# Six of eight blocks of the second feed-forward product by seven half-size products in each layer

## The chip, the cores and the metric

One core of one Trainium2 chip. The metric is the device time of one execution in microseconds (us). TensorE is called PE here, VectorE DVE, ScalarE ACT, GpSimd POOL, SyncE SP, as the profile calls them.

## The reference

Two layers over 512 tokens of width 1024. Each layer is a normalised projection, a pooling mixer and an indexed attention, an output projection, and then the feed-forward part, which is the part that matters here:

```python
D_FF = 4 * D_MODEL          # 1024 -> 4096 -> 1024
for l in range(DEPTH):      # DEPTH = 2
    ...
    x = x + rms_norm(mix, g_post_mix[l])
    h = rms_norm(x, g_pre_ffn[l])
    f = jnp.square(jax.nn.relu(h @ w_ff1[l])) @ w_ff2[l]
    x = x + rms_norm(f, g_post_ffn[l])
```

All inputs are float32, and so is the output.

## The kernel before

**Exactness.** PE takes float32 rounded to a shorter form (fp32r). So every operand is kept as a high part (a copy that rounds) and a low part (the value minus the high part), and every product is three matmuls: high by high, high by low, low by high (`PASSES`, `mm3`). The high parts are copies, which either DVE or ACT may do (`copy`, a choice of the planner). The low parts are subtractions of two tensors, and `tt` gives those to DVE alone.

**Weights.** `WeightStream` loads weights in DMAs of 512 KB issued by SP, and makes tiles `ws` of high and low part from them, 128 rows by 512 columns each, in a ring of eight (`NWS`). A tile is refilled when the matmuls on it are over (`done`). Plain weights pass through `wraw` (two buffers), one copy and one subtraction a tile.

**The first feed-forward product** is cut into eight blocks of 512 hidden columns. Block 0 is a plain product (tiles `pf`). The other seven are done by seven half-size products instead of eight (`unit_products`): the 2 x 2 quarters of the weights (in `uraw`, two buffers of two quarters' worth) are combined into S1 to S4, the quarters of the activations into T1 to T4 (once a layer), and PE makes seven products into the banks `one` and `two`. For the weights of one block that is 14 tiles `ws`, so 14 copies and 14 subtractions, and 8 more additions and subtractions on DVE for S1 to S4 (tiles `usum` and `uraw`). The result of each quarter is squared after a relu (`fr`) and split into the parts of `f`, `f1h`, `f1l`.

**The second feed-forward product** is plain. Two blocks of hidden columns at a time (loop `g`, four times a layer) and for each half of the 1024 output columns, 8 chunks by 4 token tiles by 3 passes of 512 columns go into four banks `pg`, and DVE adds the banks into `facc` (the first time they are copied).

**Order.** Nothing runs in the order in which it is written. Every operation is recorded (`_Recorder`, line 372, which is why all rows of the profile carry that line), and `Planner.issue` puts the operations of each engine into a fixed order by rules on durations and latencies. On the chip each engine takes its instructions in that order and waits for semaphores.

Of the kernel before, what the change touches and what calls it, by code (L numbers as in the profile page):

```python
# [12 lines left out]
F32 = mybir.dt.float32  # L13
# [5 lines left out]
P = 128  # L19
# [16 lines left out]
NWS = 8  # L36
NRAW = 2
# [45 lines left out]
class Planner:  # L83
# [9 lines left out]
    DMA_LANDS = 1050  # L93
    CELL = 64
# [93 lines left out]
    def lag(self, ea, eb):  # L188
        if eb == "sp":
# [169 lines left out]
class _Recorder:  # L359
# [3 lines left out]
    def __getattr__(self, method):  # L363
        def call(*args, **kw):
# [4 lines left out]
            reads = [a for k, a in list(enumerate(args))[1:] + list(kw.items())  # L369
# [19 lines left out]
    def cost(self, method, args, kw, out, reads):  # L389
# [20 lines left out]
        if self.name == "pool":  # L410
            if method == "memset":
                return 50
            return (70 + 1.2 * n) if method == "tensor_scalar" else (520 if n == 1 else 50 + 2.35 * n)
        nbytes = math.prod(c for _, c in out.ap) * 4
# [3 lines left out]
class WeightStream:  # L418
# [5 lines left out]

    COMBINATIONS = ("11", "12", "S2", "S1", "S3", "S4", "22")

    def __init__(self, copy, tt, sp, raw_pool, ws_pool, unit_pool, sum_pool):
        self.copy, self.tt, self.sp = copy, tt, sp
# [53 lines left out]
    def _ahead(self):  # L482

        while self.n_load < len(self.loads):
            unit = self.loads[self.n_load][2] == "unit"
# [5 lines left out]
    def _load(self):  # L491
# [3 lines left out]
        if n == "unit":  # L495
# [43 lines left out]
    def _combine(self, k, name, w):  # L539
# [3 lines left out]

        def quarter(i, j):
            return raw[:, j, :, 256 * i:256 * i + 256]

        def v(ap):
            return ap.rearrange("p (c n) -> p c n", c=2)
# [37 lines left out]
def hymba_trunk(ctx: ExitStack, tc: tile.TileContext, x, positions, g_pre_mix, w_in, w_pool,  # L586
# [4 lines left out]
        ("pe", nc.tensor), ("act", nc.scalar), ("dve", nc.vector), ("pool", nc.gpsimd), ("sp", nc.sync))]  # L591
    ctx.enter_context(tc.manual_schedule())
# [72 lines left out]
    ws = WeightStream(copy, tt, sp, rawp, wsp, t8p, sup)  # L665
    plan = []
    for l in range(DEPTH):
# [14 lines left out]
        for g in range(4):  # L682
            for b in (2 * g, 2 * g + 1):
                p["ff1", b] = ws.add_unit(w_ff1[l], 0, 512 * b) if b else ws.add(w_ff1[l], 0, D, 512 * b, 512)
            for hf in range(2):
                p["ff2", g, hf] = ws.add(w_ff2[l], 1024 * g, 1024, 512 * hf, 512)
# [183 lines left out]
    for l in range(DEPTH):  # L870
# [261 lines left out]
        def unit_products(ids, f):  # L1132
# [21 lines left out]
            def evac(rows, cols, value, other=None):  # L1154
                r = t2("fr")[:, :512]
                if other is not None:
                    dve.tensor_tensor(r, value, other, op=OP.add)
                    value = r
                planner.either(lambda: act.activation(r, value, AF.Relu),
                               lambda: dve.tensor_scalar(r, value, 0.0, None, op0=OP.max))  # L1160
                squared(r, r)
                rv = r.rearrange("p (j n) -> p j n", j=2)
                hi = f[0][:, 2 * rows:2 * rows + 2, cols]
                copy(hi, rv)
                tt(f[1][:, 2 * rows:2 * rows + 2, cols], rv, hi.bitcast(F32), OP.subtract)
# [4 lines left out]
            evac(0, LATER, two, p1)  # L1170
# [6 lines left out]
            evac(1, SOONER, one, p5)  # L1177
            product(two, "S4", "22")
            evac(0, SOONER, two, u2)
            product(one, "22", "T4")  # L1180
            evac(1, LATER, one)

        facc = None
        for g in range(4):
            f1 = []
            for bi in range(2):
                blk = 2 * g + bi
                if bi == 0:
                    f = [c2a.tile([P, 4, S], F32R, name="f1h", tag="c2a"), c2b.tile([P, 4, S], F32R, name="f1l", tag="c2b")]
                else:  # L1190
                    f = c1p.tile([P, 2, 4, S], F32R, name="f1", tag="c1")
                    f = [f[:, 0], f[:, 1]]
                f1.append(f)
                ids = p["ff1", blk]

                def evac_f(j, ps, cols):
                    r = t2("fr")[:, :ps.shape[1]]
                    planner.either(lambda: act.activation(r, ps, AF.Relu),
                                   lambda: dve.tensor_scalar(r, ps, 0.0, None, op0=OP.max))
                    squared(r, r)  # L1200
# [3 lines left out]
                if blk == 0:  # L1204
                    for tp in (1, 0):
                        cols = slice(256 * tp, 256 * tp + 256)
                        for j in range(4):
# [70 lines left out]
```

## Time and profile before

| | us |
|---|---|
| median of 3 runs | 1189.85 (1188.28 to 1189.97) |
| profiled execution, its own time | 1189.19 |
| its span, first to last instruction | 1187.4 |
| outside the span | 1.8 |

PE is busy for 97% of the span, DVE for 81%, ACT for 50%, POOL for 3%; the mean granted PE clock is 0.992 of full speed. The feed-forward part lies at about 248 to 598 us in layer 0 and 834 to 1179 us in layer 1. In a timeline, two adjacent records of one engine can overlap: the start of the next one, not the length of a record, tells how fast the engine takes such instructions.

### The profile page before, as it was taken

How to read it: one execution, taken by the hardware profiler on the slowest of the kernel's cores; microseconds unless marked ns; L12 is line 12 of the kernel's file. 1: busy time of each engine (PE TensorE's matmuls, PEld its weight loads, DVE VectorE, ACT ScalarE, POOL GpSimd, SP SyncE). 2: the span in 40 equal slices, each digit the busy share in tenths (PEclk: the TensorE clock that was granted, in tenths of full speed). 3: DMA queues.
4: the chain of work that ended last, by engine and by line, in shares of the span. 5: the costliest groups of instructions: out<-in, count | busy, mean ns of one | idle time of the engine just before them, and what ended most of it. 6: DMA issues, size and time to landing. Idle time of an engine off the chain costs nothing.

```text
span 1187.4 us, 18436 instructions
## 1 busy us (share of the span) xinstructions
PE 1154.9 (97%) x6888; PEld 1008.9 (85%) x6888; DVE 962.8 (81%) x2134; ACT 593.5 (50%) x1279; POOL 31.5 (3%) x79
## 2 busy tenths in 40 slices
PE   6999999999999999999999999899999999999997
PEld 6988888789899898899898888777998998988985
DVE  7799999889569579577698999998994785875965
ACT  7545796687226036035275277876760440430621
POOL 2000000010000000000010000001000000000001
PEclk9999998999999999999999999999999999999999
DMA  7221222451423223223233121134542241251231
GB/s 249 71 72 36 71 72 72 142 184 66 161 74 132 95 72 132 82 71 97 60 112 89 54 72 54 54 115 134 160 141 73 71 161 54 72 177 36 72 107 71
DMA packets 62169, 115.55 MB, mean 97 GB/s; under 512 B 5248, under 2 KB 10368, under 8 KB 62080
## 3 DMA queue, kind: packets, MB, share of 16 engines
q1 hardware_dynamic: 62080, 114.38, 30.2%
q8 instruction: 54, 0.88, 0.3%
q14 instruction: 35, 0.29, 0.1%
HBM read 112.27 MB, written 2.10 MB: 96 GB/s over the span
## 4 chain that ended last, share of the span: by engine, by line
PE 61%; DVE 26%; DMA 5%; ACT 4%; issue 3%; POOL 1%; SPq 0%; DVEq 0%; ACTq 0%; POOLq 0%
PE pg L372 33%; PE one L372 9%; PE two L372 7%; DVE ws L372 6%; DVE bias L372 3%; PE pi L372 3%; PE pf L372 3%; DVE m L372 3%; DMA wraw<-in_w_out_dram 2%; DMA uraw<-in_w_ff_dram 2%; DVE mx L372 1%; PE lg L372 1%; DVE s L372 1%; PE po L372 1%; DVE pT L372 1%
## 5 line engine op out<-in xcount | busy, mean ns | idle before, releaser
L372 PE MATMUL pg<-ws,f 128*128 128x512 f32 x768 | 230.5, 394 | 0.0
L372 PE MATMUL pg<-ws,A 128*128 128x512 f32 x864 | 227.5, 401 | 0.9 <-DVE A L372 0.6
L372 ACT ACTIVATE ws<-wraw 128x512 fp32r<-128x512 f32 (+1 forms) x182 | 112.9, 632 | 183.8 <-PE pg L372 127.3
L372 DVE TENSOR_TENSOR ws<-wraw,ws 128x512 fp32r<-128x512 f32 (+1 forms) x288 | 194.4, 689 | 5.9 <-ACT ws L372 3.8
L372 PEld LDWEIGHTS pg<-ws,A 128*128 128x128 f32 x864 | 157.7, 188 | 34.3 <-DVE pn L372 1.6
L372 PE MATMUL pg<-ws,f1h 128*128 128x512 f32 x512 | 167.2, 394 | 0.5 <-ACT fr L372 0.5
L372 PEld LDWEIGHTS pg<-ws,f 128*128 128x128 f32 x768 | 141.1, 188 | 29.0
L372 PEld LDWEIGHTS pg<-ws,f1h 128*128 128x128 f32 x512 | 95.6, 188 | 22.3 <-ACT fr L372 1.0
L372 DVE TENSOR_TENSOR ws<-uraw,ws 128x512 fp32r<-128x512 f32 x168 | 111.7, 686 | 2.0 <-ACT ws L372 0.7
L372 DVE CAST ws<-wraw 128x512 fp32r<-128x512 f32 (+1 forms) x106 | 45.0, 426 | 75.2 <-PE pg L372 64.3
L372 PE MATMUL two<-A,ws 128*128 128x256 f32 x672 | 104.9, 281 | 0.0
L372 PE MATMUL pg<-ws,f1l 128*128 128x512 f32 x256 | 95.8, 393 | 0.0
L372 PEld LDWEIGHTS two<-A,ws 128*128 128x128 f32 x672 | 92.3, 188 | 1.9
L372 ACT ACTIVATE ws<-uraw 128x512 fp32r<-128x512 f32 x95 | 57.7, 627 | 67.8 <-PE pg L372 29.7
L372 ACT ACTIVATE s<-s,st 128x384 f32<-128x384 f32 (+3 forms) x118 | 64.7, 565 | 21.4 <-DVE st L372 20.8
L372 ACT ACTIVATE fr<-fr 128x512 f32<-128x512 f32 (+1 forms) x109 | 63.5, 596 | 21.0 <-DVE fr L372 20.1
L372 DVE TENSOR_TENSOR facc<-pg,facc 128x512 f32<-128x512 f32 x48 | 32.7, 688 | 46.2 <-PE pg L372 46.2
L372 DVE CAST ws<-uraw 128x512 fp32r<-128x512 f32 x73 | 30.4, 424 | 41.7 <-PE pg L372 32.6
L372 PE MATMUL pi<-ws,A 128*128 128x292 f32 x384 | 61.8, 310 | 1.1 <-DVE ws L372 0.8
L372 PE MATMUL pool<-A,ws 128*128 128x512 f32 x192 | 59.2, 405 | 0.0
L372 PEld LDWEIGHTS pg<-ws,f1l 128*128 128x128 f32 x256 | 48.0, 188 | 10.9
L372 PE MATMUL one<-A,ws 128*128 128x256 f32 x336 | 57.0, 280 | 0.0
(189 smaller groups left out, 2203.5 us busy)
## 6 DMA issues: line engine op xcount, KB each, us to landing
wraw<-in_w_ff_dram SPq DMA_DIRECT2D x72, 512.0 KB, 3.8
uraw<-in_w_ff_dram SPq DMA_DIRECT2D x56, 512.0 KB, 4.9
wraw<-in_w_out_dram SPq DMA_DIRECT2D x32, 512.0 KB, 3.7
wraw<-in_w_in_dram SPq DMA_DIRECT2D x24, 512.0 KB, 3.6
wraw<-in_w_in_dram SPq DMA_DIRECT2D x8, 584.0 KB, 4.3
wraw<-in_w_in_dram SPq DMA_DIRECT2D x16, 256.0 KB, 2.9
x<-in_x_dram SPq DMA_DIRECT2D x4, 512.0 KB, 6.5
out_dram<-x SPq DMA_DIRECT2D x8, 256.0 KB, 2.1
```

The lines of the kernel that those rows point to most:

```text
L372: lambda: getattr(self.real, method)(*args, **kw), self.port(method, out, reads))
```

## The change

In blocks 1 to 6 of each layer the second product is done by seven half-size products too; blocks 0 and 7 stay plain (`PLAIN_FF2`).

- Weights: `add_unit(..., wide=True)` loads the 512 x 1024 block of `w_ff2` into two `uraw` tiles, and the same code makes 14 tiles `ws` and S1 to S4 from it. Before, the block was 8 tiles `ws` from `wraw`.
- Activations: the squared quarters stay in float32 (`r`), four subtractions make T1 to T4 of them, and seven parts (three quarters and T1 to T4) are split into high and low, instead of four quarters. T2 and T3 are put into columns of `A` that are no longer read, T4 into a buffer of `wraw`.
- Results: `ff2_unit` runs seven products of 2 chunks by 2 token tiles by 3 passes, 84 matmuls of 512 columns instead of 96, and adds both banks of every product into `facc`: 14 additions a block, where the plain form has 8 additions for two blocks.
- Order: block b+1 of the first product is written ahead of block b of the second. The loads of two gains are moved to the end of the feed-forward part.
- `SUMMED_BY_DMA` would let a DMA make some low parts; its lists are empty, so DVE makes all of them.

```diff
     DMA_STARTS = 1170
...
-    def add_unit(self, src, r0, c0):
+    def add_unit(self, src, r0, c0, wide=False):
 
         k = len(self.loads)
         for cp in range(2):
-            self.loads.append((src, r0 + 2 * cp * P, "unit", c0, 512))
+            if wide:
+                self.loads.append((src, r0 + cp * P, "wide", c0, 1024))
+            else:
+                self.loads.append((src, r0 + 2 * cp * P, "unit", c0, 512))
         ids = {}
...
+                if n == "wide":
+                    self.sp.dma_start(t[:, k].rearrange("p c n -> p (c n)"),
+                                      src[r + 2 * k * P:r + (2 * k + 1) * P, c0:c0 + ncols])
+                    continue
...
-            return raw[:, j, :, 256 * i:256 * i + 256]
+            return raw[:, j, i] if wide else raw[:, j, :, 256 * i:256 * i + 256]
...
         def halves(value):
             self.copy(high, value)
-            self.tt(low, value, high.bitcast(F32), OP.subtract)
+            if name in self.SUMMED_BY_DMA["wide" if wide else "unit"]:
+                self.act.activation(low, high.bitcast(F32), AF.Copy, scale=-1.0)
+                self.gq.dma_start(low, value, accum_op=OP.add)
+            else:
+                self.tt(low, value, high.bitcast(F32), OP.subtract)
...
+        def ff1(b):
+            p["ff1", b] = ws.add_unit(w_ff1[l], 0, 512 * b) if b else ws.add(w_ff1[l], 0, D, 0, 512)
+
+        def ff2(b):
+            if b in PLAIN_FF2:
+                p["ff2", b] = [ws.add(w_ff2[l], 512 * b, 512, 512 * hf, 512) for hf in range(2)]
+            else:
+                p["ff2", b] = ws.add_unit(w_ff2[l], 512 * b, 0, True)
+
+        ff1(0)
+        ff2(0)
+        ff1(1)
+        for b in range(1, 8):
+            if b < 7:
+                ff1(b + 1)
+            ff2(b)
...
-        load_gain(("post_ffn", l), g_post_ffn, l)
-        if l + 1 < DEPTH:
-            load_gain(("pre_mix", l + 1), g_pre_mix, l + 1)
...
+        def split(parts, value):
+            copy(parts[0], value)
+            tt(parts[1], value, parts[0].bitcast(F32), OP.subtract)
+
...
-        for g in range(4):
-            f1 = []
-            for bi in range(2):
-                blk = 2 * g + bi
...
-                    planner.either(lambda: act.activation(r, ps, AF.Relu),
-                                   lambda: dve.tensor_scalar(r, ps, 0.0, None, op0=OP.max))
-                    squared(r, r)
-                    copy(f[0][:, j, cols], r)
-                    tt(f[1][:, j, cols], r, f[0][:, j, cols].bitcast(F32), OP.subtract)
...
+            else:
+                def place(i):
+                    return [x.rearrange("p j n -> p (j n)")[:, 512 * i:512 * i + 512].rearrange(
+                        "p (c n) -> p c n", c=2) for x in f]
+
+                r, U = {}, {}
+
+                def put(q, value):
+                    r[q] = value
+                    if q != "12":
+                        U[q] = place({"11": 0, "21": 1, "22": 2}[q])
+                        split(U[q], value)
+
+                pair = []
+
+                def room(q):
+                    if len(pair) < 2 and q in ("11", "12"):
+                        pair.append(gp.tile([P, D], F32, name="r", tag="gain"))
+                    i = ("11", "22", "12", "21").index(q)
+                    return pair[i // 2][:, 512 * (i % 2):512 * (i % 2) + 512]
+
+                unit_products(p["ff1", b], put, room)
+                U["T1"] = place(3)
+                U["T2"] = [A[:, a, 0:2, SOONER] for a in range(2)]
+                U["T3"] = [A[:, a, 2:4, SOONER] for a in range(2)]
+                tt(r["11"], r["12"], r["11"], OP.subtract)
+                split(U["T1"], r["11"])
+                tt(r["12"], r["22"], r["12"], OP.subtract)
+                tt(r["22"], r["22"], r["11"], OP.subtract)
+                tt(r["21"], r["21"], r["22"], OP.subtract)
+
+                def second_and_third():
+                    split(U["T2"], r["22"])
+                    split(U["T3"], r["12"])
+
+                def fourth():
+                    if b < 6:
+                        ws.in_use["raw"] += 1
+                        x = rawp.tile([P, 2, WMAX], F32R, name="U4", tag="wraw")
+                    else:
+                        x = t4("U4").rearrange("p (a n) -> p a n", a=2)
+                    U["T4"] = [x[:, a, :512].rearrange("p (c n) -> p c n", c=2) for a in range(2)]
+                    split(U["T4"], r["21"])
+
+                later[b] = second_and_third, fourth
+                return U
+            return f
...
+                else:
+                    for c in range(4):
+                        for t in range(NT):
+                            step(c, t)
+                        ws.done()
...
+        def ff2_unit(b, U):
+
+            ids = p["ff2", b]
+
+            def product(banks, name, other, new, *quarter):
+                for c in range(2):
+                    w = ws.get(ids[name][c])
+                    for t in range(2):
+                        for i, (a, b) in enumerate(PASSES):
+                            pe.matmul(banks[t], U[other][a][:, c, P * t:P * t + P], w[:, b, :512],
+                                      start=new and c == i == 0, stop=c == 1 and i == 2, skip_group_check=True)
+                    ws.done()
+                cs = slice(512 * quarter[0], 512 * quarter[0] + 512)
+                for t in range(2):
+                    acc = facc[:, (2, 0)[quarter[1]] + t, cs]
+                    dve.tensor_tensor(acc, banks[t], acc, op=OP.add)
+
+            one = [pm("one2"), pm("one2")]
+            two = [pq(i, "two2") for i in range(2)]
+            product(one, "11", "11", True, 0, 0)
+            product(two, "12", "21", True, 0, 0)
+            product(one, "S2", "T2", False, 0, 1)
+            two = [pq(i, "two2") for i in range(2)]
+            product(two, "S1", "T1", True, 1, 1)
+            product(one, "S3", "T3", False, 1, 1)
+            product(two, "S4", "22", False, 0, 1)
+            product(one, "22", "T4", False, 1, 0)
...
+        def finish(b):
+            later[b][0]()
+            if b < 6:
+                later[b][1]()
+
+        later = {}
+        f = {0: ff1_block(0)}
+        facc = c0p.tile([P, NT, D], F32, name="facc", tag="c0")
+        ff2_plain(0, f.pop(0))
+        f[1] = ff1_block(1)
+        finish(1)
+        for b in range(1, 8):
+            if b < 7:
+                f[b + 1] = ff1_block(b + 1)
+            if b == 6:
+                later[6][1]()
+                load_gain(("post_ffn", l), g_post_ffn, l)
+                if l + 1 < DEPTH:
+                    load_gain(("pre_mix", l + 1), g_pre_mix, l + 1)
+            if b in PLAIN_FF2:
+                ff2_plain(b, f.pop(b))
+            else:
+                ff2_unit(b, f.pop(b))
+                if b < 6:
+                    ws.in_use["raw"] -= 1
+                    finish(b + 1)
```

What the planner makes of it, in the middle of layer 0. First DVE, before, while PE runs the plain second product of group 1 and the weights of the next block of the first product begin (`ws` is a weight tile, `facc` the sum of the second product, `pg` a bank, `usum` and `uraw` the combined quarters):

```order
L372 CAST ws<-wraw 128x512
L372 TENSOR_TENSOR ws<-wraw,ws 128x512
L372 TENSOR_TENSOR facc<-pg,facc 128x512 x2
L372 TENSOR_TENSOR ws<-wraw,ws 128x512
L372 CAST ws<-uraw 128x512
L372 TENSOR_TENSOR ws<-uraw,ws 128x512
L372 TENSOR_TENSOR uraw<-usum,uraw 128x2x256
```

The same engine now, during block 1 of the second product (`one`, `two`: banks; `U`: a part of the split activations):

```order
L376 TENSOR_TENSOR facc<-two_800,facc 128x512
L376 TENSOR_TENSOR ws<-usum,ws 128x512
L376 CAST ws<-uraw 128x512
L376 TENSOR_TENSOR ws<-uraw,ws 128x512 x6
L376 TENSOR_TENSOR ws<-usum,ws 128x512
L376 TENSOR_TENSOR facc<-one_798,facc 128x512
L376 TENSOR_TENSOR facc<-one_799,facc 128x512
L376 TENSOR_TENSOR facc<-two_810,facc 128x512
L376 TENSOR_TENSOR facc<-two_811,facc 128x512
L376 TENSOR_TENSOR ws<-uraw,ws 128x512
L376 TENSOR_TENSOR usum<-uraw 128x512
L376 TENSOR_TENSOR U_769<-r,U_769 128x512
```

Before, a copy goes ahead of most subtractions and two additions into `facc` follow a whole half of a group. Now the subtractions stand in runs with few copies, four additions into `facc` stand between the last tile made of one pair of `uraw` buffers and the first of the next pair, and the sums for the next pair follow at once.

PE, before, in the second product of group 0 (`f`, `f1h`, `f1l` are split activations of two blocks):

```order
L372 MATMUL pg<-ws,f_723 128x512 x5
L372 MATMUL pg<-ws,f1l 128x512
L372 MATMUL pg<-ws,f_723 128x512 x2
L372 MATMUL pg<-ws,f1h 128x512 x2
L372 MATMUL pg<-ws,f_723 128x512
L372 MATMUL pg<-ws,f1l 128x512
L372 MATMUL pg<-ws,f_723 128x512 x4
L372 MATMUL pg<-ws,f1h 128x512 x4
```

PE now, at the end of block 1 of the second product (names with numbers are its banks) where it is mixed with block 3 of the first (`one<-A`):

```order
L376 MATMUL one_799<-ws,A 128x512
L376 MATMUL one<-A,ws 128x256 x3
L376 MATMUL two_811<-ws,f_742 128x512
L376 MATMUL one<-A,ws 128x256 x2
L376 MATMUL one_798<-ws,A 128x512
L376 MATMUL two_810<-ws,f_742 128x512 x2
L376 MATMUL one<-A,ws 128x256 x4
L376 MATMUL one_799<-ws,A 128x512
L376 MATMUL one_798<-ws,A 128x512
L376 MATMUL two_811<-ws,f_742 128x512
```

Before, runs of the second product stood alone for a whole group; now matmuls of 512 columns on two pairs of banks and matmuls of 256 columns of the next block of the first product stand among each other.

## Rows read from the trace of the kernel before

**Rows 1.** The page, busy time (share of the span) of each engine:
```profile
PE 1154.9 (97%) x6888; PEld 1008.9 (85%) x6888; DVE 962.8 (81%) x2134; ACT 593.5 (50%) x1279; POOL 31.5 (3%) x79
```

**Rows 2.** Windows: stretch, its length, busy of PE, PEld, DVE, ACT, POOL; clock, DMA:
```profile
282.00:597.00 315.00, 312.77 (x1906) 277.94 (x1905) 226.97 (x395) 112.49 (x205) 2.08 (x4) 1.00 0.30 97
866.00:1172.00 306.00, 305.47 (x1869) 272.31 (x1868) 213.00 (x373) 102.25 (x181) 0.00 (x0) 1.00 0.29 93
```

**Rows 3.** Timeline of PE: start, us, instructions merged; 256 and 512 columns:
```profile
290.87 3.01 PE L372 MATMUL two<-A,ws 128*128 128x256 f32 x24
293.72 0.28 PE L372 MATMUL one<-T4h,ws 128*128 128x256 f32 x1
...
309.56 3.18 PE L372 MATMUL pg<-ws,f 128*128 128x512 f32 x13
312.59 0.39 PE L372 MATMUL pg<-ws,f1h 128*128 128x512 f32 x1
```

**Rows 4.** Timeline of DVE in dense stretches of the first product:
```profile
371.61 0.75 DVE L372 CAST ws<-uraw 128x512 fp32r<-128x512 f32 x2
372.27 1.89 DVE L372 TENSOR_TENSOR ws<-uraw,ws 128x512 fp32r<-128x512 f32 x3
374.08 1.29 DVE L372 TENSOR_TENSOR ws<-wraw,ws 128x512 fp32r<-128x512 f32 x2
...
871.65 0.41 DVE L372 TENSOR_TENSOR f1l<-fr,f1h 128x256 fp32r<-128x256 f32 x1
871.99 0.68 DVE L372 TENSOR_TENSOR ws<-uraw,ws 128x512 fp32r<-128x512 f32 x1
872.59 1.21 DVE L372 TENSOR_TENSOR T4l<-hraw,T4h 128x1024 fp32r<-128x1024 f32 x1
873.72 1.28 DVE L372 TENSOR_TENSOR ws<-uraw,ws 128x512 fp32r<-128x512 f32 x2
```

**Rows 5.** Timeline of DVE: the last part of A in either layer:
```profile
266.29 0.68 DVE L372 TENSOR_TENSOR A<-hT,A 128x512 fp32r<-128x512 f32 x1
850.19 0.68 DVE L372 TENSOR_TENSOR A<-hT,A 128x512 fp32r<-128x512 f32 x1
```

**Rows 6.** Timeline of PE: the last matmuls of the second product, either layer:
```profile
595.02 3.02 PE L372 MATMUL pg<-ws,f 128*128 128x512 f32 x12
1173.16 5.73 PE L372 MATMUL pg<-ws,f 128*128 128x512 f32 x24
```

**Rows 7.** Waits of DVE: waited for, us in total, times, longest:
```profile
DVE ws L372 <- ACT ws L372: 4.5, 11, 1.4
DVE ws L372 <- DMA uraw<-in_w_ff_dram: 4.2, 6, 1.0
DVE f L372 <- ACT fr L372: 2.3, 7, 0.8
DVE usum L372 <- DMA uraw<-in_w_ff_dram: 2.1, 3, 0.9
```

**Rows 8.** The chain that ended last: start, us; loads between two such blocks:
```profile
352.90 4.70 DMA uraw<-in_w_ff_dram
...
436.17 6.19 DMA uraw<-in_w_ff_dram
```

**Rows 9.** Timeline of DVE behind such a load (idle before <- releaser):
```profile
937.49 0.43 DVE L372 CAST ws<-uraw 128x512 fp32r<-128x512 f32 x1 [0.34 <-DMA uraw<-in_w_ff_dram]
937.95 0.69 DVE L372 TENSOR_TENSOR ws<-uraw,ws 128x512 fp32r<-128x512 f32 x1
938.76 0.69 DVE L372 TENSOR_TENSOR usum<-uraw 128x512 f32<-128x512 f32 x1
```

**Rows 10.** Windows (as rows 2) where the granted clock of PE is under 1:
```profile
160.00:180.00 20.00, 18.63 (x111) 15.67 (x110) 19.85 (x59) 19.73 (x43) 0.23 (x2) 0.95 0.17 53
180.00:200.00 20.00, 19.69 (x95) 16.34 (x94) 18.61 (x71) 13.28 (x47) 0.00 (x0) 0.79 0.25 80
...
760.00:780.00 20.00, 16.78 (x91) 13.55 (x91) 19.24 (x72) 12.64 (x38) 0.00 (x0) 0.91 0.18 54
```

More of the change, by code (lines that the diff above doesn't have):

```diff
@@ L188, in lag @@
     def lag(self, ea, eb):
+        if ea == "gq":
+            return self.SUM_LANDS
         if eb == "sp":
@@ L368, in call @@
                 writes.append(args[7])
-            reads = [a for k, a in list(enumerate(args))[1:] + list(kw.items())
+            reads = ([out] if kw.get("accum_op") is not None else []) + [a for k, a in list(enumerate(args))[1:] + list(kw.items())
                      if isinstance(a, bass.AP) and k not in ("out", "accum_out") and all(a is not w for w in writes)]
@@ L1152, in kept, with evac @@
                 return k
[L1154 to L1160, printed above, removed]
-                squared(r, r)
[L1162 to L1165, printed above, removed]
+            def evac(q, value, other=None):
+                r = room(q)
+                relu_squared(r, value, other)
+                put(q, r.rearrange("p (c n) -> p c n", c=2))
             product(one, "11", "11", True)
@@ new lines, in ff1_block, with put @@
+        def ff1_block(b):
+            if b % 2:
+                whole = c1p.tile([P, 2, 4, S], F32R, name="f1", tag="c1")
+                f = [whole[:, 0], whole[:, 1]]
+            else:
+                f = [c2a.tile([P, 4, S], F32R, name="f1h", tag="c2a"),
+                     c2b.tile([P, 4, S], F32R, name="f1l", tag="c2b")]
+            if b == 0:
+                ids = p["ff1", 0]
+                for tp in (1, 0):
+                    cols = slice(256 * tp, 256 * tp + 256)
+                    for j in range(4):
+                        bank = pq(j, "pf")[:, :256]
+                        for kc in range(KC):
+                            w = ws.get(ids[kc])
+                            mm3(bank, lambda a: w[:, a, j * P:(j + 1) * P],
+                                lambda b: A[:, b, kc, cols], kc == 0, kc == KC - 1)
+                            if tp == 0 and j == 3:
+                                ws.done()
+                        r = t2("fr")[:, :256]
+                        relu_squared(r, bank)
+                        split([x[:, j, cols] for x in f], r)
+            elif b in PLAIN_FF2:
+                def put(q, r):
+                    k, cols = int(q[0]) - 1, (LATER, SOONER)[int(q[1]) - 1]
+                    split([x[:, 2 * k:2 * k + 2, cols] for x in f], r)
+                unit_products(p["ff1", b], put, lambda q: t2("fr")[:, :512])
+            else:
[37 more added lines that the diff above has]
+            return f
@@ L1220, in hymba_trunk, with ff2_plain @@
+        def ff2_plain(b, f):
             for hf in range(2):
[L1221 removed]
+                ids = p["ff2", b][hf]
                 cs = slice(512 * hf, 512 * hf + 512)
                 banks = [pg() for _ in range(NT)]
[L1224 removed]
                 def step(c, t):
                     w = ws.get(ids[c])
[L1228 to L1229 removed]
@@ L1231, in hymba_trunk @@
-                for c in range(4 if last else KC):
+                    mm3(banks[t], lambda a: f[a][:, c, tok(t)], lambda b: w[:, b, :512], c == 0, c == 3)
+                if b == 7 and hf == 1:
                     for t in range(NT):
-                        step(c, t)
-                    ws.done()
-                if last:
-                    for t in range(NT):
-                        for c in range(4, KC):
+                        for c in range(4):
                             step(c, t)
```

76 lines of the change are left out of this document (29 added, 47 removed).

## The prediction

> **What bounds the kernel now.** I read the page first: PE is busy for 97% of the span and DVE for 81% [rows 1]. Then the windows of the two feed-forward stretches: PE 312.8 of 315 us and 305.5 of 306 us, DVE 227.0 and 213.0, ACT 112.5 and 102.3 [rows 2]. So in the stretch that the change touches PE sets the time, DVE has 30% to spare and ACT more than half. The change takes work from PE and gives work to DVE, so the question is whether the 30% is enough.
>
> For that I need the pace of both engines, from starts in the timeline. PE: 24 matmuls of 256 columns from 290.87 to 293.72, 0.119 us each; 13 of 512 columns from 309.56 to 312.59, 0.233 us each [rows 3]. DVE: three subtractions of 512 columns from 372.27 to 374.08, 0.603 us each; two copies from 371.61 to 372.27, 0.33 us each; 256 columns in 0.34 us, 1024 in 1.13 us [rows 4].
>
> **PE's part of the change.** A block of the second product has 84 matmuls of 512 columns, not 96. In 12 blocks (six a layer) that removes 144, or 144 x 0.233 = 33.6 us. All of it lies on PE's path today, so a DVE that kept up would give 1189.2 - 33.6 = 1155.6 us.
>
> **DVE's part.** I count tensor-tensor operations of 512 columns a block, which DVE alone can do. Before, first product: 14 low parts of weights, 8 sums for S1 to S4, 3 additions of banks, 4 low parts of the result, 29; second product: 8 low parts and 4 additions into facc, 12; together 41. After: first product 14 + 8 + 3, and 4 subtractions for T1 to T4 and 7 low parts, 36; second product 14 + 8 + 14 additions, 36; together 72. One block of both products then costs DVE 72 x 0.603 = 43.4 us with no copy at all. PE needs 168 x 0.119 + 84 x 0.233 = 39.6 us for it after the change, and 42.4 us before (96 in place of 84). So **DVE becomes the bound**, by 3.8 us a block against the new PE, and by 1.0 us a block against the old one. Copies can go to ACT, which is busy for a third of these stretches [rows 2]; the order of the changed kernel puts most of them there.
>
> **The sum without stalls.** The order gives the exact list on DVE from the last part of A ahead of the feed-forward part to the last low part made from uraw. Layer 0: 470 of 512 columns, 43 copies, 7 of 1024, 6 of 256, 3 copies of a bank, 3 small ones: 283.4 + 14.2 + 7.9 + 2.0 + 1.8 + 0.9 = 310.2 us. Layer 1: 472, 41, 7, 6, 1, 3: 309.5 us. The part of A is issued at 266.29 and 850.19 us, so with its own 0.6 us the lists start at 266.9 and 850.8 [rows 5]; nothing ahead of that place is changed in amount. Behind the last low part PE still has 78 matmuls in layer 0 and 72 in layer 1, 18.2 and 16.8 us. PE would end at 266.9 + 310.2 + 18.2 = 595.3 us and at 850.8 + 309.5 + 16.8 = 1177.1 us. Today it ends at 598.0 and 1178.9 us [rows 6]. A DVE without a single stall gains 2.7 + 1.8 = 4.5 us: 1189.2 - 4.5 = **1184.7 us** is the floor by DVE. Against the profiled execution's own 1189.19 us; the median of the runs is 0.7 us higher.
>
> **Stalls.** DVE takes its list in order, so what it waits for now lands on the end. The zone has 26 half blocks by seven products (7 and 6, twice); before there were 14. Today's waits of DVE in such half blocks, on ACT's high parts (4.5 and 2.3 us) and on loads of uraw (4.2 and 2.1 us) [rows 7], come to 13.1 / 14 = 0.94 us each.
>
> The load part is a turnaround: both uraw buffers are used up together, and the next pair arrives later, by 4.70 to 6.19 us in the four such places of the chain [rows 8]. The changed order leaves 8 operations of 512 columns, 4.8 us, between the last use of most buffers and the first use of what is loaded next, where before 5 or 6 stood. So the load costs 0 to 1.4 us a half block. Waits too short for the table come on top: behind a load the copy-to-subtraction step took 0.46 us in place of 0.33, and the next step 0.81 in place of 0.60 [rows 9], 0.34 us. From below only the waits on ACT count, (4.5 + 2.3) / 14 = 0.49 us; from above 0.49 + 1.4 + 0.34 = 2.2 us. I take 0.94 + 0.34 = 1.3 us, the rate that rows of the same kind of work show. 26 x 1.3 = 33.8 us, between 12.7 and 57. Waits of DVE on PE (the largest today) should vanish, as PE will be the late one.
>
> 1184.7 + 33.8 = **1218.5 us**, forecast 1218: slower by 2.4%.
>
> **Edits that I cost at nothing.** The loads of gains now stand behind the last weight loads on SP; the plain block 7, 96 x 0.233 = 22.4 us of PE, covers them, and without cover a late one would cost about one load, 5 us, once a layer. The bytes loaded are the same. The additions into facc hold banks of the products, but the order mixes them with matmuls of the next block, which use other banks; if PE waits there, it does so inside time that it loses to DVE anyway.
>
> **Rival 1, PE stays the bound (faster).** The eight tiles ws let DVE run ahead by about 8 x 1.4 = 11 us of matmuls, and if that and the plain blocks absorbed the surplus, the 33.6 us would show: 1155.6 us, or anything from there to 1187. Against it: the surplus is 6 x 3.8 = 23 us a layer and the lead can be spent once; and the floor above already contains the plain blocks. Chance 0.07.
>
> **Rival 2, no change.** DVE is as late as PE was: stalls of only 2 to 7 us in all, under 0.27 us a half block. It needs every load hidden and fewer waits on ACT than today. Chance 0.06.
>
> **Rival 3, the clock (slower still).** PE will have some 3.8 + 2.6 = 6.4 us of gaps a block. After a stretch in which PE waited, the granted clock was 0.95 and 0.79 in two windows of 20 us, and 0.91 in another [rows 10]: a loss of 1.0 + 4.2 = 5.2 us, and of 1.8 us. If the gaps come in one piece at each turnaround and each costs 5.2 us, a half block takes PE 19.8 + 5.2 = 25.0 us, against DVE's 21.7 + 0.9 (84 copies in 30 half blocks) + 1.3 = 23.9: 1.1 us more in 26 half blocks, 29 us, 1247 us. It decides from a loss of 4.1 us a turnaround; at 1.8 us it costs nothing. For it: the weights come from DVE in a burst of six, then nothing for a turnaround. Against it: the ring holds eight tiles, and in the feed-forward windows with small gaps the clock was 1.00 [rows 2]. [...] Chance 0.13.
>
> **Rival 4, DVE's operations stop overlapping.** Three subtractions in a row stand 0.603 us apart, while one record is 0.68 us long [rows 4]: they overlap by 0.08. If the longer runs of the changed order lost that, 942 operations by 0.08 us would add 75 us to the forecast: 1294 us. Nothing in the trace shows such a loss where DVE has operations ready, so the chance is 0.03. [...]
>
> **How the numbers follow.** DVE as the bound with stalls of 0.5 to 2.2 us a half block (1197 to 1242 us): 0.71, forecast 1218. Rival 1: 0.07. Rival 2: 0.06. Rival 3: 0.13. Rival 4: 0.03. The range goes from 1197, the least stalls, to 1250, half of rival 3, and holds about 0.78. What a measurement can tell from no change is about 0.2%, 2.4 us. Faster: 0.07; same: 0.06; slower: 0.87.
>
> **What would show it.** In the windows after, DVE near 95% and PE near 90% of a stretch from the first block by seven products to block 7; PE waiting for DVE ws at the head of its waits, where no such wait of note is today; each turnaround of uraw about 5 us on DVE's own timeline with four additions into facc in it; ACT under 65%. Granted clock 1.00 there, or rival 3. Wrong if DVE has idle time that ends with PE in these stretches (rival 1), if starts of subtractions stand more than 0.62 us apart in runs (rival 4), or if the feed-forward part ends before 595 us in layer 0.

## The result and the profile after

The changed kernel takes 1242.84 us (median, 1239.98 to 1245.2) against 1189.14 us of the kernel before in the same runs: a ratio of 1.0451, 95% interval [1.0425, 1.0476], 53.7 us slower. Its profiled execution took 1241.9 us, with a span of 1240.1 us.

The page, busy time of each engine (answers to [rows 1]), and shares of the chain that ended last by engine:

```profile
PE 1153.1 (93%) x6744; PEld 995.6 (80%) x6744; DVE 1153.0 (93%) x2448; ACT 701.9 (57%) x1461; POOL 34.5 (3%) x79
...
DVE 46%; PE 37%; DMA 9%; ACT 4%; issue 3%; POOL 1%; SPq 0%; DVEq 0%; ACTq 0%; POOLq 0%
```

DVE has 190 us more to do and PE is no longer the engine without gaps. Windows from the last part of A to the last low part from `uraw` in each layer (columns as [rows 2]):

```profile
267.00:603.00 336.00, 308.90 (x1887) 272.05 (x1886) 314.85 (x535) 168.43 (x297) 0.11 (x1) 0.97 0.27 90
881.00:1215.00 334.00, 310.32 (x1884) 272.30 (x1884) 313.50 (x532) 170.64 (x302) 0.00 (x0) 0.97 0.26 89
```

Where [rows 2] had PE at 99% and DVE at 70 to 72%, DVE is now at 94%, PE at 92% and ACT at 50%. The places at which the prediction's sum begins and ends, in DVE's timeline (as [rows 5]) and then in PE's (as [rows 6]):

```profile
266.84 0.69 DVE L376 TENSOR_TENSOR A<-hT,A 128x512 fp32r<-128x512 f32 x1
...
601.65 0.68 DVE L376 TENSOR_TENSOR ws<-uraw,ws 128x512 fp32r<-128x512 f32 x1
...
880.54 0.68 DVE L376 TENSOR_TENSOR A<-hT,A 128x512 fp32r<-128x512 f32 x1
...
1214.17 0.68 DVE L376 TENSOR_TENSOR ws<-uraw,ws 128x512 fp32r<-128x512 f32 x1
```

```profile
618.13 3.04 PE L376 MATMUL pg<-ws,f 128*128 128x512 f32 x12
...
1219.59 11.27 PE L376 MATMUL pg<-ws,f 128*128 128x512 f32 x48
```

So, with 0.6 us for each first and last operation, DVE's list runs from 267.44 to 602.25 us and from 881.14 to 1214.77 us: 334.8 and 333.6 us. PE ends at 621.17 and 1230.86 us, behind the list by 18.9 and 16.1 us. What DVE waited for, first layer and second:

```profile
DVE ws L376 <- DMA uraw<-in_w_ff_dram: 6.9, 7, 1.6
DVE ws L376 <- ACT ws L376: 5.3, 8, 2.3
DVE usum L376 <- DMA uraw<-in_w_ff_dram: 2.7, 4, 1.1
DVE ws L376 <- PE one L376: 2.5, 2, 2.2
DVE ws L376 <- PE pg L376: 2.0, 1, 2.0
DVE facc L376 <- PE pg L376: 0.5, 1, 0.5
DVE facc L376 <- PE two L376: 0.3, 1, 0.3
DVE ws L376 <- PE two L376: 0.2, 1, 0.2
```

```profile
DVE ws L376 <- DMA uraw<-in_w_ff_dram: 6.7, 7, 1.5
DVE ws L376 <- ACT ws L376: 5.0, 9, 2.1
DVE ws L376 <- PE one L376: 3.1, 3, 2.5
DVE ws L376 <- PE pg L376: 2.0, 2, 1.3
DVE facc L376 <- PE two L376: 1.4, 2, 1.0
DVE ws L376 <- DMA wraw<-in_w_ff_dram: 0.7, 1, 0.7
DVE ws L376 <- PE two L376: 0.5, 1, 0.5
DVE facc L376 <- PE pg L376: 0.2, 1, 0.2
```

Loads: 9.6 and 7.4 us. High parts from ACT: 5.3 and 5.0. Matmuls that had still to release a weight tile or fill a bank: 5.5 and 7.2. And PE's two longest waits in layer 0's stretch:

```profile
PE two L376 <- DVE facc L376: 7.7, 3, 2.7
PE two L376 <- DVE ws L376: 5.4, 4, 2.0
```

PE waits for DVE, as foreseen, but more for additions into `facc`, which have to empty its banks, than for weights.

### The profile page after: what moved, and what is told of

It is laid out like the page before. It is cut to its first block, busy times and chain, and to the rows that moved or that the text cites. A ratio compares the mean times of both kernels' runs of the same rounds, so it can differ in the third digit from the quotient of the medians.

```text
span 1240.1 us, 18754 instructions
## 1 busy us (share of the span) xinstructions
PE 1153.1 (93%) x6744; PEld 995.6 (80%) x6744; DVE 1153.0 (93%) x2448; ACT 701.9 (57%) x1461; POOL 34.5 (3%) x79
## 4 chain that ended last, share of the span: by engine, by line
DVE 46%; PE 37%; DMA 9%; ACT 4%; issue 3%; POOL 1%; SPq 0%; DVEq 0%; ACTq 0%; POOLq 0%
DVE ws L376 15%; PE pg L376 12%; PE one L376 9%; DMA uraw<-in_w_ff_dram 8%; PE two L376 7%; DVE uraw L376 4%; DVE facc L376 4%; DVE bias L376 3%; DVE m L376 3%; PE pi L376 2%; DVE r L376 2%; PE pf L376 1%; DVE mx L376 1%; DVE s L376 1%; PE po L376 1%
## 5 line engine op out<-in xcount | busy, mean ns | idle before, releaser
L376 ACT ACTIVATE ws<-uraw 128x512 fp32r<-128x512 f32 x240 | 146.4, 626 | 183.2 <-DMA uraw<-in_w_ff_dram 76.6
L376 DVE TENSOR_TENSOR ws<-uraw,ws 128x512 fp32r<-128x512 f32 x312 | 203.2, 683 | 10.9 <-ACT ws L376 10.2
L376 DVE TENSOR_TENSOR ws<-wraw,ws 128x512 fp32r<-128x512 f32 (+1 forms) x192 | 129.9, 687 | 2.3 <-ACT ws L376 1.6
L376 PE MATMUL one<-ws,A 128*128 128x512 f32 x288 | 83.3, 409 | 1.0 <-DVE A L376 0.5
L376 PE MATMUL two<-ws,f 128*128 128x512 f32 x216 | 68.7, 426 | 16.7 <-DVE facc L376 7.6
L376 DVE TENSOR_TENSOR uraw<-uraw 128x512 f32<-128x512 f32 x104 | 69.6, 683 | 0.1
L376 PEld LDWEIGHTS one<-ws,A 128*128 128x128 f32 x288 | 55.8, 199 | 14.0 <-DVE ws L376 1.3
L376 DVE TENSOR_TENSOR facc<-one,facc 128x512 f32<-128x512 f32 x96 | 63.0, 680 | 1.0 <-PE one L376 1.0
L376 PEld LDWEIGHTS pi<-ws,A 128*128 128x128 f32 x384 | 55.9, 199 | 4.2 <-ACT A L376 2.1
L376 PEld LDWEIGHTS one<-A,ws 128*128 128x128 f32 x336 | 52.6, 188 | 6.3 <-ACT ws L376 0.4
```

The lines of the kernel that those rows point to most:

```text
L376: lambda: getattr(self.real, method)(*args, **kw), self.port(method, out, reads))
```

## The experiments

All in one table: the time, how far it is above the kernel before in the same runs, and the profiled span in five parts: up to the last part of A in layer 0; from there to the end of its feed-forward matmuls; attention and the rest of the way to the last part of A in layer 1; its feed-forward matmuls; the end. "Blocks" are those with half-size second products in each layer. Only e5_pad_same and e10_less_pe keep the changed kernel's order on DVE and ACT, and on PE but for the matmuls added or left out. All other kernels were planned anew, so their differences hold the order's share too.

| kernel | us | above before | start | ff 0 | attention | ff 1 | end |
|---|---|---|---|---|---|---|---|
| before | 1189.1 | | 266.3 | 331.7 | 252.2 | 328.7 | 8.5 |
| changed, blocks 1 to 6 | 1242.8 | 53.7 | 266.8 | 354.3 | 259.4 | 350.3 | 9.2 |
| e1_plain, no block | 1190.7 | 1.2 | 266.6 | 328.9 | 254.9 | 328.5 | 9.3 |
| e5_pad_same | 1254.2 | 65.1 | 268.7 | 356.3 | 258.1 | 362.3 | 9.2 |
| e10_less_pe | 1237.3 | 49.1 | 268.4 | 351.7 | 258.9 | 347.5 | 9.2 |
| e3_relief | 1220.4 | 30.9 | 267.1 | 346.5 | 261.3 | 336.1 | 9.2 |
| e7_noload | 1220.7 | 31.6 | 265.9 | 348.5 | 253.1 | 341.3 | 9.3 |
| e8_three | 1219.7 | 31.5 | 267.7 | 349.6 | 256.6 | 333.6 | 9.6 |
| e4_pad | 1230.9 | 41.4 | 268.5 | 354.1 | 256.3 | 340.9 | 9.3 |
| e6_seed | 1238.1 | 49.0 | 268.7 | 356.4 | 258.2 | 343.6 | 9.2 |
| e9_pool | 1234.4 | 45.4 | 264.9 | 349.4 | 257.5 | 352.6 | 9.6 |
| e2_alternate, 1, 3, 5 | 1178.6 | -10.9 | 262.1 | 324.6 | 253.6 | 325.3 | 9.3 |
| e11_alternate_seed, 1, 3, 5 | 1190.0 | 1.7 | 268.1 | 327.8 | 254.4 | 328.1 | 9.2 |
| e12_four, 1, 2, 4, 6 | 1202.6 | 14.3 | 267.7 | 333.3 | 257.8 | 331.8 | 9.3 |

**The new order alone.**

```diff
-PLAIN_FF2 = (0, 7)
+PLAIN_FF2 = (0, 1, 2, 3, 4, 5, 6, 7)
```

> Only the new order: all eight blocks of both layers take the plain second product (144 matmuls of 512 columns more than the changed kernel, the 12 blocks' half-size products and their sums gone), but the weights, the first product and the second product are recorded block by block as in the changed kernel. Theory (VectorE's longer list is what costs the changed kernel its 53 us): VectorE has 413 fewer additions and subtractions than the changed kernel's 1221, TensorE has as many matmuls as before the change and is the bound again, so the time is that of the kernel before, 1189 us, within 6 us either way (the halves hand back PSUM banks twice as often). Rival (the block-wise order, with its handing back of banks and its loads, costs the time, not the arithmetic): 1225 to 1245 us.

Measured 1190.71 us, a ratio of 1.0011 [1.0002, 1.002]. Written block by block, with the gains loaded late, the kernel takes 1 us more; the half-size products, with the order that the planner makes of them, cost the other 52.

**TensorE's work, more and less, all else in place.** In one kernel the third pass of a group is followed by a further one, in the other it is left out, at the same places of an otherwise identical order.

```diff
-                            pe.matmul(banks[t], ...
+                            (padded if c == 0 and i == 2 else pe).matmul(banks[t], ...
```

> The changed kernel, every instruction of every engine in its own order, with a repeated pass (high data, low weights) put right behind the last pass in half of the matmul groups of the half-size second product: 168 matmuls of 512 columns more, 39.1 us at 0.233 us, and nothing else (so the output is not the reference's: one term is counted twice). The padded kernel of the run before was 12 us faster than the changed kernel, but had another planned order. Theory (TensorE's clock, which falls where it waits for VectorE, is part of the stalls, and the padding keeps it up): 1228 to 1240 us, granted clock at 0.99 or above in both stretches. Rival (the other planned order made the 12 us): 1243 to 1270 us, clock up or not.

> The changed kernel, every other instruction in its own order, without the third pass (low data, high weights) in half of the matmul groups of the half-size second product: 168 matmuls of 512 columns less, 39.1 us at 0.233 us (part of the sum is left out). It is the other side of the run with 168 matmuls more, which took 11 us more. Theory (VectorE's list sets the end; TensorE's work counts only where VectorE waits for it, some 7 us a layer): 0 to 14 us less, 1229 to 1243 us. Rival 1 (TensorE sets the end): 30 to 39 us less, 1205 to 1213 us. Rival 2 (the clock: less work for TensorE lowers it, and what is left takes longer): clock below 0.97 and 1240 us or more.

(The further pass of the first one is low by low, as in e4_pad below; its text names another one, and nothing is counted twice.) Measured 1254.15 and 1237.34 us: 39.1 us more of PE's work cost 11.4 us, 39.1 us less gave back 4.7 us. So only 0.29 and 0.12 of PE's work reach the end, and DVE's list sets the time. The first of the two went against its theory, and its rival has the time: the clock, 0.984 in place of 0.977 over the span, did not pay. In the second, the window of layer 0 shows the same DVE time in nearly the same length, with PE busy for 12 us less:

```profile
268.00:620.00 352.00, 315.05 (x1888) 271.37 (x1887) 332.82 (x568) 179.78 (x324) 3.50 (x4) 0.98 0.27 91
```

The same stretch of the changed kernel:

```profile
267.00:621.00 354.00, 326.90 (x1968) 286.51 (x1966) 332.77 (x568) 179.46 (x323) 3.51 (x4) 0.98 0.27 91
```

**VectorE's work, less.**

```diff
             self.copy(high, value)
+            if wide and name in ("S3", "S4"):
+                self.act.activation(low, value, AF.Copy)
-            if name in self.SUMMED_BY_DMA["wide" if wide else "unit"]:
+            elif name in self.SUMMED_BY_DMA["wide" if wide else "unit"]:
```

> The changed kernel with the low parts of the combinations S3 and S4 of the second product's weights not computed: ScalarE writes a copy into their place (so the output is not the reference's). That takes 48 subtractions of 512 columns from VectorE, and the planner hands it 34 conversions of 0.33 us in return. Theory (VectorE's list sets the end of both stretches): 48 x 0.603 - 34 x 0.33 = 18 us less, 1225 us, 12 to 20 us less if stalls shift a little. Rival (TensorE's own work at its lower clock, or the loads, set the end): 0 to 6 us less.

Measured 1220.38 us, 22.8 us less relative to before, for 18 us off the list. So what DVE loses shows in the time, where of PE's work 0.12 to 0.29 did. That it was more than the 18 us is not to be read: this kernel has another order, which alone can move the time by 5 us and more (below).

**The reloads.** First half of them left out, then all of them covered by a third buffer.

```diff
+        if n == "wide":
+            self.raw[self.n_load] = self.raw[self.n_load - 2]
+            self.n_load += 1
+            return
```

> The changed kernel without the loads of the second product's half-size weights: its combinations are made again from what the first product's combinations left in the same buffers (so the output is not the reference's). The work of all engines stays; of 26 reloads of the two buffers a layer, 12 are left, and 24 of the 52 half-block loads of both layers wait for nothing. Theory (the stall of 1.9 us per half block is mostly the turnaround of a buffer through its reload): 24 x 1.9 = 45 us at most, VectorE's listed waits for these loads (9.6 us a layer, about half of them at second-product loads) at least 10 us: 1243 less 10 to 45, taken 1215 us. Rival (the stalls come from the two engines waiting for each other, with the clock, and the load's wait only shows where they fall): 0 to 8 us less, 1235 to 1243 us.

```diff
-    t8p = ring("t8p", 2)
+    t8p = ring("t8p", 3)
...
-    t2p = ring("t2p", 6)
+    t2p = ring("t2p", 4)
...
-            if self.in_use[kind] >= (2 if unit else NRAW) or unit and not self.units_allowed:
+            if self.in_use[kind] >= (3 if unit else NRAW) or unit and not self.units_allowed:
```

> The changed kernel with three buffers for half-size weights in place of two; the room comes from the ring of 512-column results (fr, p1, u2, p5), four buffers in place of six. Nothing is left out. Without half of the reloads the changed kernel took 22 us less. Theory (the turnaround of a buffer through its reload is what those 22 us were): with a third buffer nearly all of the turnarounds are hidden, 20 to 35 us less, 1208 to 1223 us, and the waits of VectorE for these loads in the two stretches fall from 9.6 us to under 3 us. Rival (the smaller ring holds VectorE and ScalarE up as much, or the loads only show where two coupled engines wait): 1230 to 1250 us.

Measured 1220.67 and 1219.74 us, 22.1 and 22.2 us less. The first expectation counted buffers where the stall of 1.9 us is one of a pair: 12 pairs of 26 lose their reload, 12 x 1.87 = 22.4 us. That agrees in size, but 6.3 us of the gain lie in the attention part, so the agreement is in part luck. With three buffers the waits for loads are down from 17.0 to 0.2 us; DVE's waits in layer 0 and layer 1, from the top:

```profile
DVE ws L376 <- PE pg L376: 2.8, 3, 2.1
DVE ws L376 <- PE two L376: 2.7, 4, 0.8
DVE ws L376 <- ACT ws L376: 2.5, 6, 0.9
```

```profile
DVE ws L376 <- PE one L376: 2.8, 1, 2.8
DVE ws L376 <- ACT ws L376: 2.2, 5, 0.9
DVE ws L376 <- PE pg L376: 1.6, 3, 1.0
```

By the paces of [rows 4] its two lists are 314.5 and 304.2 us; they took 329.9 and 314.1 us (267.68 to 597.53, 873.86 to 1187.95). Stalls of 15.4 + 9.9 = 25.3 us are left, against 48.7 us. So about half of the stalls went with the reload, in two kernels of different order. Waits on high parts from ACT fell too, from 10.3 to 4.7 us; those on PE stayed, 8.6 and 5.4 us in all. What the order did to the 22 us was not separated.

**How much is the order's luck.**

```diff
-                        for i, (a, b) in enumerate(PASSES):
+                        for i, (a, b) in enumerate(PASSES + ((1, 1),) * (c == 0)):
```

> The changed kernel with a fourth pass (low by low) in half of the matmul groups of the half-size second product: 14 matmuls of 512 columns more in each of 12 blocks, 168 x 0.233 = 39.1 us of TensorE work, nothing more for VectorE. Theory (VectorE's list sets the end, TensorE has 335 - 310 = 25 us of room in each layer's stretch): the 19.6 us a layer fit the room for the most part, 0 to 12 us more, 1243 to 1255 us, and the granted clock in the stretches rises. Rival (TensorE, with its clock, sets the pace): 35 to 45 us more, 1280 us.

```diff
-    SEED = 53
+    SEED = 54
```

> The changed kernel with another seed of the planner's noise, nothing else: another order of the same work. It says how much of a few microseconds is the order's. Theory (the 7 us that the attention part lost against the kernel before are the order's luck, the stalls are not): 1235 to 1250 us, with the attention part between 250 and 262 us. Rival (the attention part loses by the change itself): attention part again 257 to 262 us, 1240 to 1246 us.

Measured 1230.85 and 1238.06 us. The padded kernel ran 12 us faster than the changed one, where both expectations had it slower. It has the same extra work on PE as e5_pad_same and is 23.7 us faster than that one, mostly in layer 1's stretch; they differ in the planned order. The clock was 0.994 over its span and 1.00 in both of its feed-forward stretches, against 0.977 and 0.98 in the changed kernel. The padding alone, with the order held, brought it to 0.99 and 0.98 in the stretches and the time up; so the 12 us need the other order, and how much of them the clock gave back is not shown. Another seed moved layer 1's stretch by 6.7 us; its attention part took 258.2 us again, as the rival had it, while the whole time was below the rival's range. So in these kernels, where DVE and PE are busy for 92 to 95% of the span, the order decides some 5 to 24 us.

**Four subtractions a block on GpSimd.**

```diff
-                tt(r["11"], r["12"], r["11"], OP.subtract)
+                pool.tensor_tensor(r["11"], r["12"], r["11"], op=OP.subtract)
```

(and the three below it likewise)

> The changed kernel with the four sums of the first product's results per block (r, 512 columns each, 48 in all) on GpSimd instead of VectorE, and nothing left out. Planner gives VectorE 29 conversions less besides. [...] Rival (the r sums lie in VectorE's waits, or GpSimd's longer latency holds up the second product): 1238 to 1250 us.

Measured 1234.42 us, 8.4 us less, which is below the rival's range. DVE's list is shorter by 48 x 0.603 + 29 x 0.33 = 38.5 us, so if it alone set the end, the kernel would take 1204 us; the author forecast 1205 to 1225 us, with room for DVE being slowed, which was the author's estimate. GpSimd takes the work, at 2.08 us a subtraction, so that DVE "alone can do" such operations, as the prediction says, holds for the program's `tt` and not for the chip. But DVE's largest group got slower, 751 ns each in place of 683. Groups of instructions, POOL's and DVE's largest, and DVE's largest in the changed kernel:

```profile
L376 POOL TENSOR_TENSOR r<-r 128x512 f32<-128x512 f32 x48 | 99.9, 2081 | 517.0 <-DVE f1l L376 151.5 <-ACT r L376 129.1 <-DVE f L376 125.2
...
L376 DVE TENSOR_TENSOR ws<-uraw,ws 128x512 fp32r<-128x512 f32 x312 | 225.8, 751 | 20.3 <-ACT ws L376 17.6 <-PE one L376 2.2
```

```profile
L376 DVE TENSOR_TENSOR ws<-uraw,ws 128x512 fp32r<-128x512 f32 x312 | 203.2, 683 | 10.9 <-ACT ws L376 10.2
```

The same 312 subtractions became 22.6 us longer, and their waits 9.4 us. The order is another one here too.

**Fewer such blocks.**

```diff
-PLAIN_FF2 = (0, 7)
+PLAIN_FF2 = (0, 2, 4, 6, 7)
...
-        finish(1)
+        if 1 in later:
+            later[1][0]()
...
+            if b in later:
+                later[b][1]()
```

> Half of the change: the half-size second product in blocks 1, 3 and 5 of each layer only, blocks 0, 2, 4, 6 and 7 plain. Theory (the bound is whichever of VectorE and TensorE has more to do over a few blocks): a pair of one such block and one plain one has 113 VectorE operations of 0.603 us, 68.1 us, against 82 us of matmuls, so TensorE stays the bound and 6 blocks x 12 matmuls x 0.233 us = 16.8 us come off the kernel before: 1172 us; locally such a block still asks 43.4 us and two reloads of VectorE against 39.6 us of TensorE, so up to 6 x 7 us may come back: 1172 to 1190 us, taken 1177. Rival 1 (each such block costs what it costs in the changed kernel, 53 us over 12, whatever stands beside it): 1189 + 6 x 4.4 = 1216 us. Rival 2 (the block-wise order costs the time): 1225 to 1245 us.

With another seed:

> The kernel with the half-size second product in blocks 1, 3 and 5, with another seed of the planner's noise: another order of the same work, nothing left out. Another seed of the changed kernel gave 4.8 us less there, with 6.7 us in the second layer's stretch alone. Theory (order counts where two engines with nearly the same work wait for each other, and little where TensorE leads): 1176 to 1181 us. Rival (order is worth the same in all versions): 1172 or 1184 us and beyond.

With four blocks (`PLAIN_FF2 = (0, 3, 5, 7)`):

> The half-size second product in blocks 1, 2, 4 and 6 of each layer, plain in 0, 3, 5 and 7; with three such blocks (1, 3, 5) it took 1178.6 us. Two blocks more in all are 24 matmuls less, 5.6 us of TensorE, and 54 VectorE operations more, 32.6 us, 16.3 a layer on stretches in which VectorE is busy 287 of 318 us. Theory (TensorE stays the bound as long as VectorE has room): 303 of 315 us leave VectorE about the share at which it set the time of the changed kernel, so the gain is gone: 1177 to 1190 us, taken 1181. Rival (TensorE alone counts): 1173 us. Rival (each further block costs 4.4 us as in the changed kernel): 1187 us.

Measured 1178.63, 1189.97 and 1202.61 us: ratios of 0.9905 [0.9891, 0.992], 1.0014 [1.0001, 1.0026] and 1.0116 [1.0086, 1.0146]. The first beats both kernels and came within 2 us of its expectation, but that is not a law: with another seed the gain is gone, as the rival of that expectation had it. Of the 12.7 us between the two profiled spans, 6.0 lie ahead of the first feed-forward part, where nothing but the order differs. The two feed-forward parts gave 10.5 us of the 16.8 us of matmuls with one seed, 4.5 with the other. Four blocks fell outside all three values. Windows of layer 0's feed-forward part, with three blocks, then with four:

```profile
262.00:586.00 324.00, 321.59 (x2001) 286.00 (x2000) 292.92 (x506) 152.41 (x272) 3.14 (x4) 1.00 0.30 101
```

```profile
268.00:601.00 333.00, 324.43 (x1993) 287.10 (x1992) 307.62 (x532) 159.78 (x288) 2.69 (x4) 0.99 0.29 97
```

With three blocks PE is at 99% and DVE at 90%; with four, PE at 97% and DVE at 92%: neither is full, they wait for each other. Which of its blocks do that (1 and 2 are neighbours) was not tried, nor was another order of these four, so a part of the 24 us between three and four blocks can be the order's.

## Why the prediction was right, and where it was off

**DVE becomes the bound: right.** 39 us of PE's work either way moved the time by 5 to 11 us; 18 us off DVE's list gave 23 us, with another order; without the half-size products the kernel written in the same way runs at the old time. Rival 1 and rival 2 are out by the time itself. One sign that the prediction gave for rival 1, idle time of DVE that ends with PE, came true all the same (below).

**The sum without stalls: right in its counts.** The trace has the operations that were counted, 470 and 472 of 512 columns on two tensors, at the same pace: 310.2 and 309.5 us of list by [rows 4], and 18.2 and 16.8 us of PE behind it, of which 18.9 and 16.1 were seen.

**The stalls: the term that was too small.** 24.6 + 24.1 = 48.7 us were seen, 1.87 us in each of 26 half blocks (a block of one of the two products), where 33.8 us, 1.3 each, were forecast; the upper bound was 2.2. By the waits above, over 26:

| | forecast | measured |
|---|---|---|
| loads | 6.3 / 14 = 0.45 | 17.0 / 26 = 0.65 |
| ACT's high parts | 6.8 / 14 = 0.49 | 10.3 / 26 = 0.40 |
| PE, first 37 us | 0 | 10.2 / 26 = 0.39 |
| PE, later | 0 | 2.5 / 26 = 0.10 |
| too short for the table | 0.34 | 8.7 / 26 = 0.33 |

The step that failed lets DVE be the bound from the last part of A on: "the floor above already contains the plain blocks", and DVE's waits on PE "should vanish, as PE will be the late one". In plain block 0, the first of each stretch, PE was still the bound. Windows of layer 0 and layer 1 there, and DVE's three longest waits for PE in them (start, us, idle before and what ended it):

```profile
285.00:304.00 19.00, 19.00 (x103) 16.27 (x102) 13.55 (x24) 4.57 (x7) 0.00 (x0) 1.00 0.00 1
900.00:919.00 19.00, 19.00 (x104) 16.32 (x103) 12.94 (x23) 3.40 (x6) 0.00 (x0) 1.00 0.00 1
```

```profile
297.09 0.43 DVE L376 CAST ws<-uraw 128x512 fp32r<-128x512 f32 x1 [2.19 <-PE one L376]
303.15 0.78 DVE L376 CAST ws<-uraw 128x512 fp32r<-128x512 f32 x2 [2.01 <-PE pg L376]
...
911.74 0.43 DVE L376 CAST ws<-uraw 128x512 fp32r<-128x512 f32 x1 [2.51 <-PE one L376]
```

PE has no gap and the full clock, and DVE is busy for 71 and 68%: it waits for matmuls that have still to release a tile of the ring of eight. Up to 304 and 919 us these waits come to 5.0 and 5.2 us; in all the rest of the two stretches they are 0.5 and 2.0. So they are a price at the start of each layer's stretch and no rate of the half blocks. Without them 38.5 / 26 = 1.48 us a half block are left, against 1.3. The same 5.0 and 5.2 us stand in e10_less_pe, which takes work off PE only behind that place; no run took work off PE in block 0. The loads cost 5.3 us more than at their forecast rate, and with the third buffer nearly all of their 17.0 us went; ACT's high parts cost 2.3 us less.

**Nothing ahead of that place is changed: right in amount, not in time.** From the end of layer 0's matmuls to the last part of A in layer 1 it took 259.4 us, not 252.2: 7.2 us that no step had. With 14.9, 0.5 at the start and 0.7 at the end they make the 23.4 us between 1218.5 and 1241.9. The first 20 us of that part, before and after:

```profile
598.00:618.00 20.00, 18.95 (x147) 18.29 (x146) 18.34 (x37) 15.25 (x37) 3.55 (x5) 1.00 0.43 136
```

```profile
621.00:641.00 20.00, 17.06 (x115) 16.17 (x115) 18.77 (x39) 14.57 (x34) 5.28 (x5) 0.91 0.53 163
```

PE does 115 matmuls, not 147: it is busy for 1.9 us less, and at 0.91 of the clock 20 us are worth 1.8 us less. A likely reason, which no run tested: DVE comes late to the normalisation, as it was busy throughout the 23 us ahead of that, where before it had room; before and after:

```profile
575.00:598.00 23.00, 23.00 (x105) 18.68 (x104) 17.97 (x34) 9.05 (x23) 1.97 (x3) 1.00 0.27 79
```

```profile
598.00:621.00 23.00, 23.00 (x104) 18.50 (x103) 22.93 (x43) 13.60 (x31) 3.40 (x3) 1.00 0.36 115
```

That accounts for 3.7 of 7.2 us at most; the rest is open. The gains, which now load late, are not it: in layer 0 they are issued at 598.15 and 601.15 us, and the first operations of DVE that read them, at 607.65 and 612.04, do not wait for them. The kernels with all six blocks, e7_noload apart, lie between 256.3 and 261.3 us there, those with none or three blocks at 252.2 to 254.9. But two seeds of one program differ by 6.0 us in the part ahead of all feed-forward work, so that much could also be the order's.

**The range: met, in part by luck.** With stalls alone the prediction allowed 1197 to 1242 us, and 1241.9 is the very end of that: 7.2 us lie where it had no term, and the room above 1242 was there for rival 3. Another order of the same work took 1238.1 us.

**Rival 3, the clock: seen, not the main cause.** In the stretches the clock fell, two windows of 20 us:

```profile
480.00:500.00 20.00, 15.44 (x78) 12.75 (x77) 20.00 (x35) 9.82 (x18) 0.00 (x0) 0.93 0.23 71
1000.00:1020.00 20.00, 16.46 (x78) 13.46 (x79) 18.83 (x33) 9.28 (x17) 0.00 (x0) 0.91 0.33 105
```

The mean granted clock was 0.93 and 0.91 there. PE had been waiting for DVE, which was at 94 to 100%: waits of 2.75 and 3.34 us for additions into `facc` ended at 496.63 and 1011.86. Behind them matmuls of 512 columns started 0.43 us apart (three from 497.48 to 498.76, four from 1014.08 to 1015.78), ahead of them 0.23 us (seven from 491.16 to 492.80, nine from 1006.05 to 1008.13). What PE lost there lay mostly in its own room: with 39 us less to do and the same clock of 0.977, the time fell by 5 us. So a clock below 1.00, which the prediction gave as the sign of this rival, did not tell it from the forecast.

**Rival 4: out.** In the changed kernel's long runs on DVE the starts stay 0.60 us apart; a wait for a load ends this one:

```profile
425.92 0.69 DVE L376 TENSOR_TENSOR facc<-one,facc 128x512 f32<-128x512 f32 x1
426.52 0.68 DVE L376 TENSOR_TENSOR r<-r 128x512 f32<-128x512 f32 x1
427.12 0.69 DVE L376 TENSOR_TENSOR facc<-one,facc 128x512 f32<-128x512 f32 x1
428.94 0.69 DVE L376 TENSOR_TENSOR usum<-uraw 128x512 f32<-128x512 f32 x1 [1.14 <-DMA uraw<-in_w_ff_dram]
```

## What to carry to other kernels

Count what a change takes from the full engine and what it gives to the next one per block of work, and where the second sum exceeds the first, apply it to fewer blocks: three of eight gained 1% in one order and nothing in another, six lost 4.5%. Let the new bound's list begin only where the old bound ends: at the edge of the changed stretch, where the work is as before, the engine that was full still held the other up here, by 5 us a layer. And before a few microseconds are put down to an edit, run another order of the same work: here a seed alone moved the time by 5 and by 11 us.

## What the runs showed of the hardware beyond that

In e9_pool, the kernel with four subtractions a block on GpSimd, DVE's subtractions of two tensors in SBUF took 1.08 us on average beside one of GpSimd's, and 0.68 us elsewhere. DVE's timeline and POOL's at the same place:

```profile
413.44 3.48 DVE L376 TENSOR_TENSOR ws<-uraw,ws 128x512 fp32r<-128x512 f32 x2
...
422.75 1.28 DVE L376 TENSOR_TENSOR facc<-one,facc 128x512 f32<-128x512 f32 x2
```

```profile
413.36 3.01 POOL L376 TENSOR_TENSOR r<-r 128x512 f32<-128x512 f32 x2 [35.91 <-DVE f L376]
...
423.00 1.29 POOL L376 TENSOR_TENSOR r<-r 128x512 f32<-128x512 f32 x1 [2.52 <-ACT ws L376]
```

Two subtractions with both operands in SBUF took 3.48 us, not the usual 1.28, beside two of GpSimd's; two additions with one operand in a bank of PSUM took 1.28 us beside another. Over the whole of that trace, 54 of the 312 subtractions `ws<-uraw,ws` ran beside one of GpSimd's and took 1.08 us on average, the others 0.68; five additions into `facc` with an operand in a bank that ran beside one took 0.68. All 96 additions `facc<-one` took 679 ns on average, and 680 ns in the changed kernel. From these rows the author's estimate is that GpSimd would have taken work off DVE cheaply here only while DVE reads a bank; five additions are few, and no run arranged that.
